# The last output block of a decoder layer: its left half scaled on ScalarE and added in memory to a bias that was stored beforehand

## The chip, the cores and the metric

The kernel runs on one core of one Trainium2 chip. A core has five engines that run their own instruction streams: TensorE (PE in the profile, its weight loads PEld), VectorE (DVE), ScalarE (ACT), GpSimd (POOL) and SyncE (SP, which here only issues transfers). Sixteen DMA engines move data between HBM and the on-chip memory; a transfer is issued from the queue of SP, ACT or POOL. The metric is the device time of one launch in microseconds (us); lower is better. Times of the kernel before: median 613.67 us of three runs (613.48 to 613.99).

## The reference, cut to what matters

One decoder layer with 512 tokens and a model width of 1024: a combined projection, a retention group and a sparse attention group, an output projection with a layer norm, and a gated feed-forward block with a second layer norm. All of it in float32. Only its last lines matter here:

```python
def layer_norm(x, g, b):
    mu = jnp.mean(xf, axis=-1, keepdims=True)
    var = jnp.mean(jnp.square(xf - mu), axis=-1, keepdims=True)
    y = (xf - mu) * lax.rsqrt(var + LN_EPS)
    return (y * g + b)
...
    ffn = (jax.nn.silu(gate) * up) @ w_down
    return layer_norm(DEEPNORM_ALPHA * x + ffn, ln_ffn_gain, ln_ffn_bias)
```

Each output element is `(x - mean) * gain * rstd + bias`, where the mean and `rstd = 1/sqrt(var + eps)` belong to a token (a row), and gain and bias to a column.

## The kernel before

The 512 tokens are four blocks of 128 (`NB = 4`), a token on each of the 128 partitions, and the width of 1024 lies in two halves, `cl` (columns 0 to 511) and `cr` (512 to 1023). A tile `y[b]` of 128x1024 holds the running sum of block `b`; the trace calls it `x`. The tile `gf` (`gbf` in the trace) holds two rows repeated on all partitions: gain in `gf[:, 0]`, bias in `gf[:, 1]`. It is loaded some 40 us before the end. The whole program is scheduled by hand: each engine does its instructions in the order in which the code writes them, and semaphores between engines are set by the framework.

The down projection is accumulated in PSUM. Every product of float32 values is done as three matmuls (`mm3`, lines 94 to 96) from split high and low parts. The left halves of all blocks are finished early. At the end the right halves follow, block after block: for block `b` the products with the last four chunks of weights (`last4`, 24 matmuls) are added into `right[b]` (`dr` in the trace). Then VectorE adds the sum to `y` (`add_to`, line 1377), takes statistics of the right half (`stat`, line 1380), combines them (`moments`, line 1387), and normalizes.

For the blocks 0, 1 and 2, `rstd_of` adds eps on VectorE (line 471) and has GpSimd raise the result to the power -0.5 (line 472). Meanwhile VectorE does `shift_gain` over the 1024 columns (line 1396: subtract the mean, multiply by the gain). Then come two VectorE instructions of 512 columns that multiply by `rstd` and add the bias (line 1578), each followed by its store, issued from SP.

Block 3, the last, has its right half cut into two quarters of 256 columns, so that the first quarter's sum and statistics are done while the matmuls of the second quarter (`dc` in the trace) run. Its root is taken on ScalarE (`rstd_act`, line 1392) while VectorE does `shift_gain`; then VectorE takes the reciprocal (line 1598) and does the scale and bias in two pieces, 640 columns stored from ACT's queue and 384 columns stored from SP's (lines 1600 and 1601). After its last store SP waits for all transfers one after the other (line 1661), and a barrier of all engines ends the program.

GpSimd also issues transfers that add to their destination (`accum_op=ALU.add`). In this kernel these always add one on-chip tile to another, as in `g_sum2` (line 887).

Of the kernel before, what the change touches and what calls it, by code (L numbers as in the profile page):

```python
# [9 lines left out]
F32 = mybir.dt.float32  # L10
F32R = mybir.dt.float32r
I32 = mybir.dt.int32
AF = mybir.ActivationFunctionType
ALU = mybir.AluOpType

P = 128
S = 512
D = 1024
KT = D // P
NB = S // P  # L20
# [33 lines left out]
def hybrid_layer_kernel(ctx: ExitStack, tc: tile.TileContext, xT, x, pos, w0, wf, wt, wo,  # L54
                        wgu, wd, gng, lmg, lmb, lfg, lfb, ident_d, cols_d, masks_d, decay_d, out):
    nc = tc.nc
    V, A, G, T = nc.vector, nc.scalar, nc.gpsimd, nc.tensor
# [5 lines left out]
    sp = ctx.enter_context(tc.tile_pool(name="sp", bufs=6))  # L63
# [15 lines left out]
    def dma(dst, src):  # L79
        nc.sync.dma_start(dst, src)  # L80
# [387 lines left out]
    def rstd_of(var, n):  # L468
        e = sp.tile([P, 4], F32, tag="ve", name="ve")
        r = sp.tile([P, 4], F32, tag="rs", name="rs")  # L470
        V.tensor_scalar(e[:, :n], var, EPS, None, op0=ALU.add)  # L471
        G.tensor_tensor(r[:, :n], e[:, :n], half[:, :n], op=ALU.pow)  # L472
        return r
# [365 lines left out]
    Q = 2 * P  # L839
# [407 lines left out]
    def conv_w(c, k):  # L1247
        if k == 10 and c == 0:
            wprep((c, k), d10)
        else:  # L1250
            t, i = (r5b, 2) if k == 10 else (draw[c, k // 2], 2 * (k % 2))
            wprep((c, k), [t[:, i:i + 2].rearrange("p k c -> p (k c)")])
# [17 lines left out]
    def d_mm(acc, c, m, b, first, last, cs=slice(0, S)):  # L1270
        wh, wl = dw[c, m]
        for k in range(2):
            h, l = dh[m, k]
            bs = slice(b * P, b * P + P)
            ws = slice(k * S + cs.start, k * S + cs.stop)
            mm3(acc, h[:, bs], l[:, bs], wh[:, ws], wl[:, ws], first and k == 0, last and k == 1, skip_group_check=True)
# [92 lines left out]
    y = x1  # L1369
    cl, cr = slice(0, S), slice(S, D)  # L1370
# [5 lines left out]
    def add_to(b, cs, acc):  # L1376
        V.tensor_tensor(y[b][:, cs], y[b][:, cs], acc, op=ALU.add)

    def stat(b, i, cs):
        V.bn_stats(stats[b][:, i], y[b][:, cs])  # L1380
# [4 lines left out]
    def moments(b, n=2):  # L1385
        mv = sp.tile([P, 2], F32, tag="lmv", name="fmv")
        V.bn_aggr(mv, stats[b][:, :n])
        return mv

    def rstd_act(var):  # L1390
        e = sp.tile([P, 4], F32, tag="ve", name="ve")
        A.activation(e[:, :1], var, AF.Sqrt, bias=eps)
        return e

    def shift_gain(b, mv):
        V.scalar_tensor_tensor(y[b], in0=y[b], scalar=mv[:, 0:1], in1=gf[:, 0], op0=ALU.subtract, op1=ALU.mult)

    def prepare_down():
        conv_w(0, 0)
# [82 lines left out]
    gf = None  # L1482
    for i in range(18):
# [26 lines left out]
        elif i == 10:  # L1510
# [3 lines left out]
            gf = big.tile([P, 2, D], F32, tag="s8", name="gbf")  # L1514
# [51 lines left out]
        d_mm(right[b], 1, 10, b, b >= 2, True)  # L1566
    conv_w(1, last4[3])

    for b in range(NB - 1):
        for i in last4:  # L1570
            d_mm(right[b], 1, i, b, False, i == last4[-1])
        add_to(b, cr, right[b])
        stat(b, 1, cr)
        mv = moments(b)
        r = rstd_of(mv[:, 1:2], 1)
        shift_gain(b, mv)
        for cs in (cl, cr):
            V.scalar_tensor_tensor(y[b][:, cs], in0=y[b][:, cs], scalar=r[:, 0:1], in1=gf[:, 1, cs],
                                   op0=ALU.mult, op1=ALU.add)
            dma(out[b * P:(b + 1) * P, cs], y[b][:, cs])  # L1580

    b = NB - 1
    Q2 = slice(Q, S)
# [9 lines left out]
    stat(b, 2, c2)  # L1593
    mv = moments(b, 3)
    e = rstd_act(mv[:, 1:2])
    shift_gain(b, mv)
    r = sp.tile([P, 4], F32, tag="rs", name="rs")
    V.reciprocal(r[:, :1], e[:, :1])
    for cs, queue in ((slice(0, 640), nc.scalar), (slice(640, D), nc.sync)):
        V.scalar_tensor_tensor(y[b][:, cs], in0=y[b][:, cs], scalar=r[:, 0:1], in1=gf[:, 1, cs], op0=ALU.mult, op1=ALU.add)  # L1600
        queue.dma_start(out[b * P:b * P + P, cs], y[b][:, cs])


# [61 lines left out]
```

## Time and profile before

| what | value |
|---|---|
| median of the runs | 613.67 us (613.48 to 613.99) |
| the profiled execution | 613.35 us |
| its span, first to last instruction | 611.6 us |
| outside the span | 1.75 us |
| PE busy | 601.7 us, 98% of the span |
| DVE, ACT, POOL busy | 518.7, 350.6, 182.5 us |
| last matmul starts | 603.90 us |
| last VectorE instruction | 607.70 us |
| last store issued (SP) | 608.34 us, 192 KB, 2.3 us to landing |

Times in rows are counted from the span's start. PE is busy nearly everywhere, so for the most part a stage is worth what it does to PE. The last 7.4 us, after the end of the last matmul, are an exception: there PE has nothing left to do, and VectorE and the stores set the end. In a timeline row stand start, length, engine, line, operation, the output and its inputs, and the shapes; a bracket says how long the engine had been idle and who released it. "SPq", "ACTq" and "POOLq" are the engines' queues, where transfers are issued and waits happen. A transfer's time to landing counts from its issue.

### The profile page before, as it was taken

The page shows a single profiled execution, that of the slowest core. Times are in us where ns is not written, and L with a number is a line of the kernel's source. Part 1 is how long each engine was busy: PE and PEld are TensorE (multiplying, and loading weights), DVE is VectorE, ACT ScalarE, POOL GpSimd, SP SyncE. Part 2 cuts the span into 40 slices and gives each one's busy share as a digit, 9 for nine tenths or more (in the row PEclk, how much of TensorE's full clock was granted, in tenths as well). Part 3 has the DMA queues.
Part 4 walks back from the last instruction along what each step waited for, and adds up shares of the span by engine and source line. Part 5 has one row for each costly group of instructions (what it writes and reads, how often), then busy time and mean ns, then how long its engine had stood idle before and what let it go on. Part 6 is the DMA issues. An engine that isn't in the chain of part 4 may idle for free.

```text
span 611.6 us, 9201 instructions
## 1 busy us (share of the span) xinstructions
PE 601.7 (98%) x3256; PEld 519.1 (85%) x3256; DVE 518.7 (85%) x943; ACT 350.6 (57%) x619; POOL 182.5 (30%) x197
## 2 busy tenths in 40 slices
PE   9999999999999999999999999999999999999995
PEld 7987888888888878889998888888888988888884
DVE  6788976898987887989999989889898878977856
ACT  5454444433352755877757776767777685648300
POOL 0136732331363000342013444435353421214011
PEclk9999999999999999999999999999999999999999
DMA  8875774689553873497248888888878879689602
GB/s 295 239 235 148 156 182 124 151 206 224 135 127 104 295 254 129 113 245 144 87 147 206 179 194 200 176 208 165 208 150 198 178 226 205 155 228 295 201 34 103
DMA packets 48014, 110.77 MB, mean 181 GB/s; under 512 B 8880, under 2 KB 23280, under 8 KB 42464
## 3 DMA queue, kind: packets, MB, share of 16 engines
q1 hardware_dynamic: 25232, 77.02, 38.2%
q0 software_dynamic: 22432, 32.71, 32.0%
q8 instruction: 25, 0.41, 0.3%
q10 hardware_dynamic: 304, 0.46, 0.3%
q14 instruction: 21, 0.17, 0.1%
HBM read 74.52 MB, written 2.10 MB: 125 GB/s over the span
## 4 chain that ended last, share of the span: by engine, by line
PE 86%; DVE 5%; POOL 2%; DMA 2%; issue 2%; ACT 1%; SPq 1%; POOLq 0%; DVEq 0%; ACTq 0%
PE ga L921 10%; PE ga L923 5%; PE gc L921 5%; PE ga L929 5%; PE pt L95 4%; PE pt L94 4%; PE pt L96 3%; PE pf L96 3%; PE pf L94 3%; PE pf L95 3%; PE gc L923 3%; PE gb L921 3%; PE dl L94 2%; PE dl L96 2%; PE dl L95 2%; PE gc L929 2%
## 5 line engine op out<-in xcount | busy, mean ns | idle before, releaser
L86 ACT CAST wh<-raw 128x1024 fp32r<-128x1024 f32 x44 | 46.0, 1048 | 40.6 <-PE pt L96 16.2
L872 POOL DMA_DIRECT2D t<-t x34 | 29.1, 857 | 85.7 <-DVE t L1005 57.3
L94 PE MATMUL pf<-xh,wh 128*128 128x512 f32 x128 | 50.1, 392 | 0.3 <-DVE rt L235 0.3
L96 PE MATMUL pf<-xh,wl 128*128 128x512 f32 x128 | 50.0, 390 | 0.2 <-DMA wl<-raw 0.2
L95 PE MATMUL pf<-xl,wh 128*128 128x512 f32 x128 | 49.9, 390 | 0.0
L872 POOL DMA_DIRECT2D w<-w x34 | 39.0, 1184 | 32.5 <-DVE w L955 23.9
L472 POOL TENSOR_TENSOR rs<-ve,half 128x1 f32<-128x1 f32 (+1 forms) x11 | 11.9, 1083 | 109.4 <-DVE ve L471 109.2
L91 DVE TENSOR_TENSOR wl<-raw,wh 128x1024 fp32r<-128x1024 f32 x26 | 31.6, 1222 | 12.1 <-ACT wh L86 12.0
L94 PE MATMUL pt<-wh,xh 128*128 128x512 f32 (+1 forms) x96 | 38.5, 401 | 0.0
L95 PE MATMUL pt<-wl,xh 128*128 128x512 f32 (+1 forms) x96 | 37.0, 386 | 0.0
L96 PE MATMUL pt<-wh,xl 128*128 128x512 f32 (+1 forms) x96 | 36.7, 382 | 0.0
L89 POOL DMA_DIRECT2D wl<-raw x18 | 15.8, 876 | 49.9 <-ACT wl L88 39.6
L96 PEld LDWEIGHTS pf<-xh,wl 128*128 128x128 f32 x128 | 24.0, 188 | 5.7 <-DMA wl<-raw 0.6
L94 PEld LDWEIGHTS pf<-xh,wh 128*128 128x128 f32 x128 | 24.0, 188 | 5.2 <-issue 0.7
L95 PEld LDWEIGHTS pf<-xl,wh 128*128 128x128 f32 x128 | 24.1, 188 | 4.5
L434 DVE MAX8 m<-score 128x8 f32<-128x256 f32 (+2 forms) x48 | 26.8, 558 | 1.0
L435 DVE MATCH_REPLACE8 score<-m,score 128x256 f32<-128x256 f32 (+2 forms) x48 | 26.0, 542 | 0.0
L417 ACT ACTIVATE lg<-lg 128x256 f32<-128x256 f32 (+2 forms) x24 | 10.9, 474 | 23.1 <-PE lg L416 21.2
L89 POOL DMA_DIRECT2D slot<-hu x9 | 10.9, 1336 | 37.9 <-ACT slot L88 37.2
L96 PEld LDWEIGHTS pt<-wh,xl 128*128 128x128 f32 x96 | 18.0, 188 | 3.3
L423 DVE SCALAR_TENSOR_TENSOR score<-lg,iw,score 128x256 f32<-128x256 f32 (+2 forms) x21 | 13.0, 618 | 9.2 <-ACT lg L417 8.2
L94 PEld LDWEIGHTS pt<-wh,xh 128*128 128x128 f32 x96 | 18.1, 188 | 2.8
(1184 smaller groups left out, 1984.1 us busy)
## 6 DMA issues: line engine op xcount, KB each, us to landing
graw<-in_wgu_dram SPq DMA_DIRECT2D x22, 1024.0 KB, 5.4
wl<-raw POOLq DMA_DIRECT2D x18, 512.0 KB, 5.2
raw<-in_wo_dram SPq DMA_DIRECT2D x8, 1024.0 KB, 4.9
raw<-in_wf_dram SPq DMA_DIRECT2D x7, 1024.0 KB, 6.5
raw<-in_wt_dram SPq DMA_DIRECT2D x6, 1024.0 KB, 5.1
r<-in_wd_dram SPq DMA_DIRECT2D x12, 512.0 KB, 5.8
w<-w POOLq DMA_DIRECT2D x34, 128.0 KB, 4.0
graw<-graw POOLq DMA_DIRECT2D x17, 256.0 KB, 3.7
```

The costliest lines, as they stand in the source:

```text
L86: A.copy(hi, src)
L89: nc.gpsimd.dma_start(lo.bitcast(F32), src, accum_op=ALU.add)
L91: eng_lo.tensor_tensor(lo, src, hi.bitcast(F32), op=ALU.subtract)
L94: T.matmul(acc, lhsT=lh, rhs=rh, start=first, stop=False, **kw)
L95: T.matmul(acc, lhsT=lh, rhs=rl, start=False, stop=False, **kw)
L96: T.matmul(acc, lhsT=ll, rhs=rh, start=False, stop=last, **kw)
L434: V.max(m8, a)
L435: V.match_replace(out=a, in_to_replace=m8, in_values=a, imm_value=TAKEN)
L872: nc.gpsimd.dma_start(t[:, :Q], t[:, Q:], accum_op=ALU.add)
L921: T.matmul(pair, lhsT=h[:, ws[k]], rhs=parts[q][:, :, k], start=first and k == 0, stop=False, skip_group_check=True)
L923: T.matmul(full[:, :Q], lhsT=l[:, ws[k]], rhs=parts[q][:, 0, k], start=False, stop=k == 3, skip_group_check=True)
L929: T.matmul(gp[n][acc], lhsT=a[:, i * S + k * P:i * S + k * P + P], rhs=parts[q][:, b, k], start=first and j == 0, stop=j == 11, skip_group ...
```

## The change

The left half of the last block no longer gets its bias on VectorE:

- Once `gf` is there, before the last blocks, SP stores the bias rows of the left half straight into the last block's left half of the output.
- Block 3's `shift_gain` is cut into halves. After the left half comes the reciprocal; then ScalarE multiplies the left half by `rstd` (a `Copy` with a scale per partition), and GpSimd issues a transfer that adds it to the stored bias, in HBM.
- Meanwhile VectorE does `shift_gain` on the right half, and scale and bias in two quarters of 256 columns, stored from ACT's queue and from SP's.
- Block 2 takes its root on ScalarE and the reciprocal on VectorE as block 3 does, not on GpSimd.

```diff
-    def shift_gain(b, mv):
-        V.scalar_tensor_tensor(y[b], in0=y[b], scalar=mv[:, 0:1], in1=gf[:, 0], op0=ALU.subtract, op1=ALU.mult)
+    def shift_gain(b, mv, cs=slice(0, D)):
+        V.scalar_tensor_tensor(y[b][:, cs], in0=y[b][:, cs], scalar=mv[:, 0:1], in1=gf[:, 0, cs], op0=ALU.subtract, op1=ALU.mult)
+
+    def inverse(e):
+        r = sp.tile([P, 4], F32, tag="rs", name="rs")
+        V.reciprocal(r[:, :1], e[:, :1])
+        return r
+
+    def scale_bias(b, r, cs, queue):
+        V.scalar_tensor_tensor(y[b][:, cs], in0=y[b][:, cs], scalar=r[:, 0:1], in1=gf[:, 1, cs], op0=ALU.mult, op1=ALU.add)
+        queue.dma_start(out[b * P:(b + 1) * P, cs], y[b][:, cs])
...
+    last = out[(NB - 1) * P:NB * P, cl]
+    dma(last, gf[:, 1, cl])
     for b in range(NB - 1):
...
-        r = rstd_of(mv[:, 1:2], 1)
-        shift_gain(b, mv)
+        if b == NB - 2:
+            e = rstd_act(mv[:, 1:2])
+            shift_gain(b, mv)
+            r = inverse(e)
+        else:
+            r = rstd_of(mv[:, 1:2], 1)
+            shift_gain(b, mv)
...
-    shift_gain(b, mv)
-    r = sp.tile([P, 4], F32, tag="rs", name="rs")
-    V.reciprocal(r[:, :1], e[:, :1])
-    for cs, queue in ((slice(0, 640), nc.scalar), (slice(640, D), nc.sync)):
-        V.scalar_tensor_tensor(y[b][:, cs], in0=y[b][:, cs], scalar=r[:, 0:1], in1=gf[:, 1, cs], op0=ALU.mult, op1=ALU.add)
-        queue.dma_start(out[b * P:b * P + P, cs], y[b][:, cs])
+    shift_gain(b, mv, cl)
+    r = inverse(e)
+    A.activation(y[b][:, cl], y[b][:, cl], AF.Copy, scale=r[:, 0:1])
+    nc.gpsimd.dma_start(last, y[b][:, cl], accum_op=ALU.add)
+    shift_gain(b, mv, cr)
+    for cs, queue in ((slice(S, S + Q), nc.scalar), (slice(S + Q, D), nc.sync)):
+        scale_bias(b, r, cs, queue)
```

How the instructions move on VectorE, after the last statistics of block 3 (`x_1_1956` is the tile of the last two blocks, `ve` the root, `rs` its reciprocal):

```order
 L1387 BN_AGGR fmv<-fst_2775 128x2
-L1396 SCALAR_TENSOR_TENSOR x_1_1956<-x_1_1956,fmv,gbf 128x1024
-L1598 RECIPROCAL rs<-ve 128x1
-L1600 SCALAR_TENSOR_TENSOR x_1_1956<-x_1_1956,rs,gbf 128x640
-L1600 SCALAR_TENSOR_TENSOR x_1_1956<-x_1_1956,rs,gbf 128x384
-L1661 UNCONDITIONAL_BRANCH
+L1396 SCALAR_TENSOR_TENSOR x_1_1956<-x_1_1956,fmv,gbf 128x512
+L1400 RECIPROCAL rs<-ve 128x1
+L1396 SCALAR_TENSOR_TENSOR x_1_1956<-x_1_1956,fmv,gbf 128x512
+L1404 SCALAR_TENSOR_TENSOR x_1_1956<-x_1_1956,rs,gbf 128x256 x2
```

The reciprocal now comes after 512 columns and not after 1024, and 512 columns of scale and bias remain on VectorE where there were 1024.

On GpSimd's queue, after the last transfers of the down projection (`slot`):

```order
 L89 DMA slot_5741<-ts_5236 128x512
-L472 TENSOR_TENSOR rs<-ve,half 128x1 x3
-L1661 UNCONDITIONAL_BRANCH
-L1661 ISA
+L472 TENSOR_TENSOR rs<-ve,half 128x1 x2
+L1613 DMA out_dram<-x_1_1956 128x512
+L1676 UNCONDITIONAL_BRANCH
+L1676 ISA
```

One of GpSimd's three powers is gone, and a transfer is its last work before the end of the program.

On SP's queue, from the last loads of weights (`draw`) on:

```order
 L80 DMA draw_1_5769<-in_wd_dram 128x2x512 x2
-L80 DMA out_dram<-x_0_1955 128x512 x4
-L80 DMA out_dram<-x_1_1956 128x512 x2
-L1601 DMA out_dram<-x_1_1956 128x384
-L1661 UNCONDITIONAL_BRANCH
+L80 DMA out_dram<-gbf 128x512
+L1405 DMA out_dram<-x_0_1955 128x512 x4
+L1405 DMA out_dram<-x_1_1956 128x512 x2
+L1405 DMA out_dram<-x_1_1956 128x256
```

The store of the bias stands behind the last loads and ahead of all other stores.

More of the change, by code (lines that the diff above doesn't have):

```diff
@@ L1574, in hybrid_layer_kernel @@
         mv = moments(b)
-        r = rstd_of(mv[:, 1:2], 1)
-        shift_gain(b, mv)
+        if b == NB - 2:
[5 more added lines that the diff above has]
+            shift_gain(b, mv)
         for cs in (cl, cr):
-            V.scalar_tensor_tensor(y[b][:, cs], in0=y[b][:, cs], scalar=r[:, 0:1], in1=gf[:, 1, cs],
-                                   op0=ALU.mult, op1=ALU.add)
-            dma(out[b * P:(b + 1) * P, cs], y[b][:, cs])
+            scale_bias(b, r, cs, nc.sync)
     b = NB - 1
```

## The prediction

> **What bounds the kernel now.** I looked at the core's span and clock first, then at the timeline after the last matmul, since only that part of the program is rewritten.
>
> ```profile
> core 0: 611.6 us, clock 0.998
> ```
>
> The clock is full, so no row below is stretched by the throttle. The timeline of the end (start, length, engine, line):
>
> ```profile
> 603.90 0.28 PE L96 MATMUL dc<-dh(1, 3)_5888,h 128*128 128x256 f32 x1
> 603.99 0.43 DVE L1380 BATCH_NORM_STATS2 fst<-x 128x6 f32<-128x256 f32 x1
> 604.33 0.41 DVE L1377 TENSOR_TENSOR x<-x,dc 128x256 f32<-128x256 f32 x1
> 604.77 0.43 DVE L1380 BATCH_NORM_STATS2 fst<-x 128x6 f32<-128x256 f32 x1
> 605.23 0.24 DVE L1387 BATCH_NORM_AGGREGATE fmv<-fst 128x2 f32<-128x18 f32 x1
> 605.50 1.28 DVE L1396 SCALAR_TENSOR_TENSOR x<-x,fmv,gbf 128x1024 f32<-128x1024 f32 x1
> 605.56 0.30 ACT L1392 ACTIVATE ve<-fmv,eps 128x1 f32<-128x1 f32 x1 [22.37 <-DVE fmv L1387]
> 606.71 0.16 DVE L1598 RECIPROCAL rs<-ve 128x1 f32<-128x1 f32 x1
> 606.90 1.42 DVE L1600 SCALAR_TENSOR_TENSOR x<-x,rs,gbf 128x640 f32<-128x640 f32 x2
> 607.82 0.38 ACTq L1601 DMA_DIRECT2D out_dram<-x  x1
> 608.34 0.33 SPq L1601 DMA_DIRECT2D out_dram<-x  x1
> ```
>
> VectorE is busy without a gap from 603.99 to 608.32, and the last store leaves 0.02 us after it. The transfers of that stretch and who waits for them:
>
> ```profile
> out_dram<-x SPq DMA_DIRECT2D x6, 256.0 KB, 2.0
> out_dram<-x ACTq DMA_DIRECT2D x1, 320.0 KB, 2.2
> out_dram<-x SPq DMA_DIRECT2D x1, 192.0 KB, 2.3
> ...
> SPq L1661 <- DMA out_dram<-x: 1.4, 2, 0.9
> ```
>
> The last store lands at 608.34 + 2.3 = 610.64, and SP has waited for it; the 0.96 us from there to 611.6 are the closing barrier. So the end is "last transfer landed + 0.96", and a term below counts only if it moves that landing.
>
> **The change part by part.**
>
> *The store of the bias.* 256 KB from SP, behind the last loads.
>
> ```profile
> 561.87 7.62 SPq L80 DMA_DIRECT2D draw<-in_wd_dram  x4
> 591.86 0.35 SPq L80 DMA_DIRECT2D out_dram<-x  x1
> ...
> 576.70 1.06 ACT L86 CAST dh(1, 2)_5860<-draw 128x1024 fp32r<-128x1024 f32 x1 [1.66 <-PE dr L96]
> ```
>
> SP's queue has over 20 us free between the last load and the first store, and ScalarE's conversions of these loads wait for PE's buffers, not for the loads. At 2.0 us a store is in HBM well before 591. Cost 0; without that cover it would be at most its 2.0 us.
>
> *Block 2's root on ScalarE.* The rows of block 2:
>
> ```profile
> 598.04 0.39 PE L96 MATMUL dr<-dh(1, 3)_5888,h 128*128 128x512 f32 x1
> 598.47 0.69 DVE L1377 TENSOR_TENSOR x<-x,dr 128x512 f32<-128x512 f32 x1 [0.55 <-PE dr L96]
> ...
> 600.16 0.15 DVE L471 TENSOR_SCALAR ve<-fmv 128x1 f32<-128x1 f32 x1
> 600.23 1.28 DVE L1396 SCALAR_TENSOR_TENSOR x<-x,fmv,gbf 128x1024 f32<-128x1024 f32 x1
> 600.46 1.45 POOL L472 TENSOR_TENSOR rs<-ve,half 128x1 f32<-128x1 f32 x1 [3.99 <-DVE ve L471]
> 601.94 1.41 DVE L1578 SCALAR_TENSOR_TENSOR x<-x,rs,gbf 128x512 f32<-128x512 f32 x2 [0.44 <-POOL rs L472]
> ```
>
> Without line 471, `shift_gain` starts at 600.16 and ends at 601.44; ScalarE's root (0.30 us after a 0.1 us handover) is hidden under it; the reciprocal takes 0.16 us, overlapping as at 606.71. Scale and bias then start near 601.56, 0.38 us earlier. Of that only a part arrives: the addition of `dc` waits for the matmul that ends at 603.90 + 0.28 = 604.18. With the handover of 0.04 us from PE (598.43 to 598.47) it starts at 604.22 and not at 604.33. **Gain 0.11 us.** The rest becomes a wait for PE.
>
> *Block 3 on VectorE.* The shapes of these instructions, grouped:
>
> ```profile
> L1578 DVE SCALAR_TENSOR_TENSOR x<-x,rs,gbf 128x512 f32<-128x512 f32 x6 | 4.2, 749 | 1.3 <-POOL rs L472 1.3
> L1600 DVE SCALAR_TENSOR_TENSOR x<-x,rs,gbf 128x640 f32<-128x640 f32 x1 | 0.9, 886 | 0.0
> L1600 DVE SCALAR_TENSOR_TENSOR x<-x,rs,gbf 128x384 f32<-128x384 f32 x1 | 0.6, 614 | 0.0
> ```
>
> 256 columns more cost 272 ns, so 512 columns take 0.75 us and 256 columns 0.48 us; independent neighbours overlap by 0.07 us. With 0.11 off every start, `shift_gain` of the left half runs 605.39 to 606.14, the reciprocal ends at 606.23, `shift_gain` of the right half ends at about 606.95, and the quarters end at 607.46 and 607.87. SP's last store therefore leaves at 607.89, 0.45 us earlier than 608.34, and would land at 610.2.
>
> *ScalarE's scaling.* No row shows a 512-column copy with a scale per partition. The nearest:
>
> ```profile
> L886 ACT ACTIVATE graw<-graw 128x512 f32<-128x512 f32 x17 | 10.8, 634 | 2.8 <-DVE gs L880 2.8
> L593 ACT ACTIVATE ast<-ast,mx 128x512 f32<-128x512 f32 x4 | 2.8, 723 | 0.0
> ```
>
> The first has a constant scale, the second an operand per partition: 0.63 to 0.72. I take 0.71. From the reciprocal 606.23 plus the 0.09 us that line 1392 needed after VectorE, it runs 606.32 to 607.03. VectorE to GpSimd took 0.15 us (600.31 to 600.46); the same here puts GpSimd's transfer at **607.18**. Behind it on GpSimd is only the end of the program.
>
> *The accumulating store.* All transfers of this kind in the trace add tile to tile on the chip. The one with the least beside it is that of line 887, issued at 319.87; its window 318:324 shows the rate in slices of 0.15 us and the time to landing:
>
> ```profile
> GB/s 55 0 0 109 0 0 0 0 0 0 0 0 0 68 184 184 143 198 96 0 0 27 191 205 205 191 191 205 191 218 123 0 0 0 437 0 109 218 109 0
> ...
> graw<-graw POOLq DMA_DIRECT2D x1, 256.0 KB, 3.3
> ```
>
> 1.3 us until bytes move, 1.4 us at some 200 GB/s, 0.5 us until it counts as landed: 3.3 us for 256 KB, against 2.0 for the plain store. Two things are added here. First, company: two plain stores of 128 KB at the rate of the present stores in the window 606:611,
>
> ```profile
> GB/s 0 0 0 0 0 0 0 0 0 0 0 0 0 0 0 0 0 0 0 0 0 164 369 369 410 430 369 410 324 369 369 381 222 12 0 0 0 0 0 0
> ```
>
> some 370 GB/s, so 0.7 us of all DMA engines; bytes move from 608.5 to 610.0 for the accumulating store, about 608.6 to 609.9 for these, so nearly all may fall on it. 0 to 0.7; I take 0.5. Second, the destination is read from HBM. The nearest row is a load of the same size:
>
> ```profile
> r2a<-in_wd_dram SPq DMA_DIRECT2D x1, 256.0 KB, 2.8
> ```
>
> If reading only lengthens the pipe, it costs what that load takes over a store, 2.8 - 2.0 = 0.8 at most, and perhaps nothing; if all of it came ahead of the addition, 2.8. I take 0.4, near the pipelined end, since the on-chip addition shows its two inputs streamed at a steady rate. Sum: 3.3 + 0.5 + 0.4 = **4.2 us**, bounds 3.3 and 6.8.
>
> So the accumulating store lands at 607.18 + 4.2 = 611.4, after SP's (610.2) and 0.75 us after what is last today. The half on ScalarE is ready 1.16 us before today's last issue, and the slower road gives back 1.9. **Sum: +0.75 us.** The profiled execution would take 613.35 + 0.75 = 614.1; the median of the runs lies 0.32 above that execution, hence 614.4.
>
> The Trainium skill ("DMA: Bandwidth & Descriptors", "Anatomy of one DMA — SWDGE (gpsimd) path") gives a transfer issued from GpSimd about 2.0 us plus its bytes at 436 GB/s. That would be 2.6 us here; line 887 took 3.3, and its steady 200 GB/s is the difference, so the trace disagrees for accumulating transfers. By the page the store lands at 609.8, SP's store is last, and the time is 613.2. The same page ("Issuing engines are not separate DMA queues") says that transfers from all queues share the same 16 DMA engines and interleave, which speaks against a third queue at the very end. The present two stores, from ACT and SP, agree: together they keep the 370 GB/s of one. By that rule the company term is the full 0.7, the landing 611.6, and the time 614.6.
>
> **Rivals.**
>
> *Hidden (0.15).* The accumulating store costs 3.3 or a little less and lands at 610.5 or before; SP's store, 610.2, or both set the end: -0.15 to -0.45 us, 613.2 to 613.5. For it: the rate of line 887 is steady. Against it: HBM must be read, and two stores lie beside it.
>
> *Serial reading from HBM (0.20), the slower side.* If the addition waits for its data from HBM, packet by packet, the store takes 3.3 + 2.8 = 6.1 us and lands at 613.3: +2.6, so 616.3. It decides from an issue-to-landing time of 4.7 on (608.34 + 2.3 + 1.23 - 607.18), where the loss passes 0.2%. For it: no transfer of this kind to HBM is in the trace. Against it: the pipelining above.
>
> *GpSimd's own closing takes over (0.20).* The rows of the end of the program have this one:
>
> ```profile
> L1661 POOLq EVENT_SEMAPHORE  x4: 17/17/17, 610.8 to 611.4; - x4
> L1661 POOLq DRAIN  x3: 46/98/4955, 600.4 to 611.3; - x3
> ```
>
> The first drain starts at 600.4 together with the last power, and lasts 4.96 us, 3.5 beyond the power's end at 601.91. Now it is hidden: it ends at 605.4, and GpSimd's first step of the barrier is at 610.8. Issuing a transfer keeps GpSimd busy for 0.86 us,
>
> ```profile
> 319.87 0.86 POOL L887 DMA_DIRECT2D graw<-graw  x1 [0.41 <-ACT graw L886]
> ```
>
> so with one as last work at 607.18 the drain ends at 611.5 (608.04 + 3.5) to 612.1 (607.18 + 4.96), and the barrier is held 0.7 to 1.3 us: 614.4 to 615.0. This would hold whatever the store takes. Against it: two later drains of GpSimd last 0.05 and 0.1 us, so the length of the first may belong to the power ahead of it.
>
> **How the numbers follow.** Forecast 0.45, hidden 0.15, serial 0.20, closing 0.20. The measurement cannot tell less than about 0.2% (1.23 us) from no change, 612.44 to 614.90. Faster by more than that needs more than the whole 0.45 of VectorE and the most favourable transfer: 0.04 of the hidden case. Within: the forecast but for 0.03, the rest of the hidden case, half of the closing case: 0.42 + 0.11 + 0.10 = 0.63. Slower: 0.03 + 0.20 + 0.10 = 0.33. The range leaves out the extreme of the serial case and half of the unlikely gain: 613.1 to 616.0; the forecast's own is 613.6 to 615.0.
>
> **What would show it.** ScalarE's 512-column row at about 0.71 us and GpSimd's transfer issued at about 607.2; VectorE's last instruction ending near 607.9; the accumulating store's time to landing (4.2; below 3.5 it is the hidden case, above 4.7 the serial one); SP's last wait for it and not for the plain stores; GpSimd's drain ending before or after that landing. Block 2's scale should start near 601.6, and the addition of `dc` at 604.2, released by PE. The forecast is wrong if the store to HBM is as quick as a plain one, or if the drain, or anything ahead of 603.9, moves the end.

## The result

The changed kernel is slower: a median of 616.56 us against 613.58 us of the kernel before in the same comparison, a ratio of 1.0051 with a 95% interval of 1.0041 to 1.0061. That is 3.0 us, outside the predicted range of 613.1 to 616.0 and on its upper side. The profiled execution took 615.75 us, with this span:

```profile
core 0: 614.0 us, clock 0.995
```

The mean clock is a little lower than the 0.998 before, but not where PE works: up to 604 us the granted clock is 1.00 in both profiles, and only in the idle end it is 0.71 here and 0.83 before.

The end of the changed kernel in the timeline, from the last matmul on:

```profile
603.86 0.28 PE L96 MATMUL dc<-dh(1, 3)_5888,h 128*128 128x256 f32 x1
604.17 0.42 DVE L1377 TENSOR_TENSOR x<-x,dc 128x256 f32<-128x256 f32 x1 [0.19 <-PE dc L96]
...
605.37 0.75 DVE L1396 SCALAR_TENSOR_TENSOR x<-x,fmv,gbf 128x512 f32<-128x512 f32 x1
606.03 0.16 DVE L1400 RECIPROCAL rs<-ve 128x1 f32<-128x1 f32 x1
606.11 0.73 DVE L1396 SCALAR_TENSOR_TENSOR x<-x,fmv,gbf 128x512 f32<-128x512 f32 x1
606.23 0.72 ACT L1612 ACTIVATE x<-x,rs 128x512 f32<-128x512 f32 x1 [0.56 <-DVE rs L1400]
606.87 0.88 DVE L1404 SCALAR_TENSOR_TENSOR x<-x,rs,gbf 128x256 f32<-128x256 f32 x2
607.24 0.90 POOL L1613 DMA_DIRECT2D out_dram<-x  x1 [10.81 <-ACT x L1612]
607.39 0.38 ACTq L1405 DMA_DIRECT2D out_dram<-x  x1
607.78 0.33 SPq L1405 DMA_DIRECT2D out_dram<-x  x1
```

The last matmul starts at 603.86, where it started at 603.90 before, so everything ahead of the end took the same time in these two profiles, and the whole 2.4 us of the spans' difference lies behind it. VectorE's last instruction ends at 607.75, 0.57 us earlier than before; SP's last store leaves 0.56 us earlier. Yet the end is later. The transfers of this end, from issue to landing:

```profile
out_dram<-x POOLq DMA_DIRECT2D x1, 256.0 KB, 4.2
out_dram<-x ACTq DMA_DIRECT2D x1, 128.0 KB, 1.9
out_dram<-x SPq DMA_DIRECT2D x1, 128.0 KB, 2.0
```

The plain stores have landed by 609.8; the accumulating one lands at 607.24 + 4.2 = 611.4. But the barrier does not follow it by 0.2 us, as it followed the last landing before (610.64, then GpSimd's first step at 610.8). The rows of the program's closing line, and last the row of SP's drain in the kernel before:

```profile
L1676 POOLq EVENT_SEMAPHORE  x4: 17/17/17, 613.3 to 613.9; - x4
L1676 SPq DRAIN  x3: 7/7/7, 611.8 to 613.5; - x3
L1676 POOLq DRAIN  x3: 46/98/5993, 607.2 to 613.7; - x3
...
L1661 SPq DRAIN  x3: 7/7/7, 610.7 to 611.0; - x3
```

(name and count, then shortest/median/longest length in ns, then the first and the last start.) GpSimd's first drain, which stands right behind its transfer, starts at 607.2 and lasts 5.99 us, to 613.2. SP has seen all landings and reaches its own drain at 611.8; GpSimd takes its first step of the barrier at 613.3, where it was at 610.8 before. This is 2.5 us, the whole difference. Not all of it is the drain. SP's own drain came 0.1 us after the last landing before and comes 0.4 us after it here (the reason is shown with the version in three pieces). So the later landing makes 0.8 us of the difference, SP's longer waits 0.3, and GpSimd's drain, for which the barrier stands from 611.8 on, 1.3. The list of who waited for whom on SP's queue has it as two rows:

```profile
SPq L1676 <- DMA out_dram<-x: 3.1, 2, 1.6
SPq L1676 <- PEq L1676: 2.0, 2, 1.5
```

The first is the wait for landings, the longest 1.6 us. The second is the barrier: SP stands in it for 1.5 us although no engine has work left. It is put down to PE, which is only the last name in the barrier; the row of GpSimd's drain shows who was late.

### The profile page after: what moved, and what is told of

Its sections match the earlier page's. It is cut to its first block, busy times and chain, and to the rows that moved or that the text cites. A ratio compares the mean times of both kernels' runs of the same rounds, so it can differ in the third digit from the quotient of the medians.

```text
span 614.0 us, 9204 instructions
## 1 busy us (share of the span) xinstructions
PE 601.4 (98%) x3256; PEld 519.1 (85%) x3256; DVE 518.8 (85%) x944; ACT 352.0 (57%) x621; POOL 182.0 (30%) x197
## 4 chain that ended last, share of the span: by engine, by line
PE 85%; DVE 6%; issue 3%; DMA 2%; ACT 1%; SPq 1%; POOL 0%; POOLq 0%; ACTq 0%; DVEq 0%
PE ga L921 10%; PE ga L923 5%; PE gc L921 5%; PE ga L929 5%; PE pt L95 4%; PE pt L94 3%; PE pt L96 3%; PE pf L94 3%; PE pf L96 3%; PE pf L95 3%; PE gc L923 3%; PE gb L921 3%; PE dl L96 2%; PE dl L94 2%; PE dl L95 2%
## 5 line engine op out<-in xcount | busy, mean ns | idle before, releaser
L472 POOL TENSOR_TENSOR rs<-ve,half 128x1 f32<-128x1 f32 (+1 forms) x10 | 10.5, 1054 | 105.8 <-DVE ve L471 105.7
```

## The experiments

A measure first. What lies before the last matmul does not take the same time in every execution (the last matmul of the profiles below starts anywhere from 603.2 to 605.7, in the two profiles of the change at 603.86 and 605.73), so spans of two profiles cannot be compared to some tenths. What was edited lies behind the last matmul, and I compare the **tail**: the span's end minus the start of the last matmul. The kernel before has 611.55 - 603.90 = 7.65 us, the change 613.99 - 603.86 = 10.13. Each tail is that of one profile; the two of the change differ by 0.07 us, so a difference of 0.1 us is not to be relied on.

| kernel | tail, us | drain ends after GpSimd's last work, us | after its transfer's landing, us | ratio to before (95%) |
|---|---|---|---|---|
| before | 7.65 | 3.5 (a power) | - | |
| the change | 10.13 | 5.1 | 1.8 | 1.0051 (1.0041 to 1.0061) |
| the change again | 10.20 | 5.1 | 1.8 | 1.0049 (1.0035 to 1.0062) |
| block 2's root alone | 7.56 | over early | - | 1.0008 (0.9999 to 1.0017) |
| plain store from SP | 7.31 | over early | - | 1.0004 (0.9994 to 1.0014) |
| before + late power | 7.85 | 3.5 | - | 1.0009 (0.9999 to 1.0018) |
| before + late small transfer | 8.20 | 3.5 | 2.5 | 1.0003 (0.9993 to 1.0013) |
| plain store from GpSimd | 8.94 | 4.1 | 1.8 | 1.0019 (1.0008 to 1.0029) |
| 64 KB added in HBM | 8.95 | 3.9 | 1.8 | 1.0027 (1.0017 to 1.0038) |
| added on the chip | 9.90 | 4.8 | 1.8 | 1.0038 (1.0023 to 1.0053) |
| one block earlier | 7.55 | over early | 1.8 | 1.0005 (0.9995 to 1.0015) |
| three pieces | 7.92 | over early | - | 1.0008 (0.9999 to 1.0017) |

**Block 2's root alone.** Added to the kernel before:

```diff
-        r = rstd_of(mv[:, 1:2], 1)
-        shift_gain(b, mv)
+        if b == NB - 2:
+            e = rstd_act(mv[:, 1:2])
+            shift_gain(b, mv)
+            r = sp.tile([P, 4], F32, tag="rs", name="rs")
+            V.reciprocal(r[:, :1], e[:, :1])
+        else:
+            r = rstd_of(mv[:, 1:2], 1)
+            shift_gain(b, mv)
```

> The kernel before with one part of the change alone: block 2 takes its root on ScalarE and its reciprocal on VectorE, not on GpSimd. Theory (GpSimd's closing drain after its late transfer costs the time): this part is innocent; block 2's scale starts near 601.5, the addition of dc near 604.2, the last store 0.1 us earlier, so 0.1 us less than before, which is not to be told from no change. Rival (moving the root disturbs something ahead of the end): up to 3 us more than before.

Measured: a tail of 7.56 us, 0.09 less than before, hardly more than two profiles of one kernel differ by; in the runs no difference that can be told. This part of the change does not cost the 2.5 us.

**The change with a plain store from SP.** It leaves the bias of that half out of the output.

```diff
-    nc.gpsimd.dma_start(last, y[b][:, cl], accum_op=ALU.add)
+    dma(last, y[b][:, cl])
```

> The change with its accumulating store replaced by a plain store from SP of the half that ScalarE scaled, so the bias of the left half of the last block is left out. Theory: GpSimd has no work after block 1, its drain is over long before the end, SP's last store leaves near 607.8 and lands near 610.0; 0.5 to 0.7 us less than before (about 613.0), some 3.5 us less than the change. Rival 1 (three stores at the end hinder each other): the last lands later than 610.6, no less than before. Rival 2 (the 3 us come from ScalarE's part, the split or the early bias store): near 616, as the change.

Measured: a tail of 7.31 us, 0.34 less than before and 2.8 less than the change. The split of VectorE's work, ScalarE's scaling, the early store of the bias and three stores at the end are all still in it, so the loss hangs on the one transfer from GpSimd. Its last work is the power of block 1, in the profile's rows for GpSimd and for the closing line:

```profile
594.92 1.46 POOL L472 TENSOR_TENSOR rs<-ve,half 128x1 f32<-128x1 f32 x1 [3.97 <-DVE ve L471]
...
L1676 POOLq EVENT_SEMAPHORE  x4: 17/17/17, 610.4 to 611.0; - x4
L1676 POOLq DRAIN  x3: 46/98/4955, 594.9 to 610.8; - x3
```

The same drain of 4.96 us ends at 599.9 here, and the barrier starts at 610.4. In the runs the 0.34 us are not to be told from no change.

**The kernel before with a late power on GpSimd, and with a late small transfer.** Each adds two lines behind the last reciprocal:

```diff
+    spare = sp.tile([P, 4], F32, tag="spare", bufs=1, name="spare")
+    G.tensor_tensor(spare[:, :1], r[:, :1], half[:, :1], op=ALU.pow)
```

> The kernel before with one more power of one column on GpSimd, of the last block's reciprocal, written to a spare tile; no transfer is added. It starts near 607.0 and ends near 608.5. Theory A (the drain is long after whatever GpSimd did last, 3.5 us beyond a power as in the kernel before): the drain ends near 612.0 and the barrier starts 1.1 us later, 1.1 to 1.2 us more than before. Theory B (only a transfer from GpSimd makes the drain at the end matter, and the 5 us before had another cause): no change.

```diff
+    spare = sp.tile([P, 4], F32, tag="spare", bufs=1, name="spare")
+    nc.gpsimd.dma_start(spare[:, :1], r[:, :1])
```

> The kernel before with one small plain transfer from GpSimd (one column, 128 words, on the chip, to a spare tile) that waits for the last block's reciprocal, so it is issued near 607.0. It lands within some 2 us, near 609. Theory A1 (the drain takes a fixed 5 us from the end of GpSimd's work of issuing): the drain ends near 613.0, 2.2 us more than before, though the transfer is small and neither goes to HBM nor adds. Theory A2 (the drain waits for the transfer to land and then 1.8 us, as in the change: 613.2 after a landing at 611.4): it ends near 610.8, no change. Rival (only accumulation to HBM costs): no change.

The late power's rows (GpSimd's timeline, then the closing line):

```profile
607.75 0.54 POOL L1600 TENSOR_TENSOR spare<-rs,half 128x1 f32<-128x1 f32 x1 [5.03 <-DVE rs L1598]
...
L1663 POOLq EVENT_SEMAPHORE  x4: 17/17/17, 611.8 to 612.5; - x4
L1663 POOLq DRAIN  x3: 46/97/4058, 607.7 to 612.3; - x3
```

The drain ends at 607.72 + 4.06 = 611.8, that is 3.5 us after the power's end at 608.3, exactly as far as in the kernel before (601.91 to 605.39). GpSimd enters the barrier as soon as it is over. So theory A holds in its mechanism: 3.5 us after GpSimd's last work, whatever it was. Its price was put too high, since the power took 0.54 us and not 1.45 (why it is shorter here was not tried): the drain ended only just after the last landing, and the tail grew by 0.20 us, not by 1.1.

The late small transfer's rows (timeline, the transfer's landing, closing line):

```profile
606.46 0.61 POOL L1600 DMA_DIRECT2D spare<-rs  x1 [5.26 <-DVE rs L1598]
...
spare<-rs POOLq DMA_DIRECT2D x1, 0.5 KB, 1.7
...
L1663 POOLq EVENT_SEMAPHORE  x4: 17/17/17, 610.7 to 611.3; - x4
L1663 POOLq DRAIN  x3: 46/98/4178, 606.4 to 611.1; - x3
```

The drain ends at 610.6. A fixed 5 us from the end of the issuing (607.07) would have given 612.1, a landing at 608.2 plus 1.8 would have given 610.0; it is 3.5 us after the issuing again. SP was at its own drain at 610.0, so the barrier waited for GpSimd, and the tail grew by 0.55 us; the runs (1.0003) do not tell that from nothing. Neither A1 nor A2 was right by itself. What fits all drains so far is the later of two times: 3.5 us after GpSimd's last work, and, in the change, 1.8 us after its transfer has landed. Three kernels were then made to tell that from its rivals.

**Which property of the transfer counts.** Each replaces the accumulating store of the change: by a plain one of the same size, by one of a quarter of the columns, and by one that adds on the chip. Each leaves the bias out of all or part of that half of the output.

```diff
-    nc.gpsimd.dma_start(last, y[b][:, cl], accum_op=ALU.add)
+    nc.gpsimd.dma_start(last, y[b][:, cl])
```

> The change with its accumulating store replaced by a plain store of the same 256 KB from GpSimd, so the bias of the left half of the last block is left out. So far GpSimd's drain ended 3.5 us after its last work in three kernels (two powers, one small transfer), but 5.1 us after it in the change. Theory L (the drain also waits for the transfer to land, and ends 1.8 us after that, as in the change: 611.4 to 613.2): landing near 610.4, drain to 612.2, span near 613.0. Theory A (adding costs the extra 1.5 us): drain to 611.6, span near 612.4. Theory S (256 KB of transfer cost it, whatever they do): drain to 613.2, span 614.0.

```diff
-    nc.gpsimd.dma_start(last, y[b][:, cl], accum_op=ALU.add)
+    nc.gpsimd.dma_start(last[:, :P], y[b][:, :P], accum_op=ALU.add)
+    dma(last[:, P:], y[b][:, P:S])
```

> The change with only 128 of the 512 columns added in HBM by GpSimd (64 KB); the other 384 are stored plainly from SP without their bias, so that part of the output lacks it. Theory L (drain ends 1.8 us after the landing, or 3.5 us after GpSimd's last work, whichever is later): landing near 610.0, drain to 611.6 to 611.8, span near 612.5. Theory A (any adding transfer costs 1.5 us more): drain to 613.2, span 614.0. Theory S (the amount): drain to 611.6.

```diff
-    nc.gpsimd.dma_start(last, y[b][:, cl], accum_op=ALU.add)
+    nc.gpsimd.dma_start(gf[:, 1, cl], y[b][:, cl], accum_op=ALU.add)
+    dma(last, y[b][:, cl])
```

> The change with GpSimd's transfer adding the scaled half to the bias tile on the chip and not to the output in HBM; SP stores the scaled half plainly, so the bias of the left half of the last block is left out of the output. Theory L: landing 3.3 to 4.0 us after 607.2, near 611.0, drain to 612.8, span near 613.6. Theory A or S: drain to 613.2, span 614.0. Theory H (only HBM as destination matters): drain to 611.6, span 612.4.

The rows of the three (GpSimd's timeline, landing, drain), first the plain store:

```profile
607.46 0.63 POOL L1613 DMA_DIRECT2D out_dram<-x  x1 [10.81 <-ACT x L1612]
...
out_dram<-x POOLq DMA_DIRECT2D x1, 256.0 KB, 3.0
...
L1676 POOLq DRAIN  x3: 46/98/4789, 607.4 to 612.7; - x3
```

Then the addition of 64 KB in HBM:

```profile
608.46 0.90 POOL L1613 DMA_DIRECT2D out_dram<-x  x1 [10.81 <-ACT x L1612]
...
out_dram<-x POOLq DMA_DIRECT2D x1, 64.0 KB, 3.0
...
L1677 POOLq DRAIN  x3: 46/98/4805, 608.4 to 613.8; - x3
```

And the addition on the chip:

```profile
608.51 0.89 POOL L1613 DMA_DIRECT2D gbf<-x  x1 [10.81 <-ACT x L1612]
...
gbf<-x POOLq DMA_DIRECT2D x1, 256.0 KB, 3.9
...
L1677 POOLq DRAIN  x3: 46/98/5761, 608.5 to 614.8; - x3
```

Landings at 610.4, 611.4 and 612.4; ends of the first drain (its start plus its longest length) at 612.2, 613.2 and 614.3. By the trace's unrounded times the drain ends 1.81 us after the landing each time, and so it does in the two profiles of the change. Plain or adding, 64 or 256 KB, HBM or on the chip make no difference beyond the landing itself. (The last matmul was later than the change's 603.86: 604.07 with the plain store, 605.08 and 605.13 with the other two, so the expected times are to be read 0.2 and 1.2 later.) That is theory L. A and S fall with the plain store: its issuing ended at 608.09, from which the 3.5 us of A give 611.6 and the 5.1 us of S 613.2, and it was 612.2; H falls with the addition on the chip, whose drain ended 4.8 us after the issuing and not 3.5.

**The same device one block earlier.** The edit of the changed kernel, cut to its core (block 3 is as in the kernel before):

```diff
-    last = out[(NB - 1) * P:NB * P, cl]
+    last = out[(NB - 2) * P:(NB - 1) * P, cl]
...
-        for cs in (cl, cr):
-            scale_bias(b, r, cs, nc.sync)
+        if b == NB - 2:
+            A.activation(y[b][:, cl], y[b][:, cl], AF.Copy, scale=r[:, 0:1])
+            nc.gpsimd.dma_start(last, y[b][:, cl], accum_op=ALU.add)
+        else:
+            scale_bias(b, r, cl, nc.sync)
+        scale_bias(b, r, cr, nc.sync)
```

> The same device one block earlier: the bias of block 2's left half is stored beforehand, that half is scaled on ScalarE and added in HBM by GpSimd; block 3 is done as in the kernel before. Theory (the loss of the change is GpSimd's closing drain after a late transfer and nothing else): the transfer leaves near 602.4, lands near 606.6, the drain ends near 608.4 and is hidden; the end is that of the kernel with block 2's root alone moved, barrier near 610.7, 0.1 us less than before: no change to be told. Rival (an accumulating store to HBM disturbs the rest, or the early bias store does): 2 us or more above before.

```profile
603.78 0.90 POOL L1595 DMA_DIRECT2D out_dram<-x  x1 [6.10 <-ACT x L1594]
...
out_dram<-x POOLq DMA_DIRECT2D x1, 256.0 KB, 3.6
...
L1677 POOLq EVENT_SEMAPHORE  x4: 17/17/17, 611.9 to 612.6; - x4
L1677 POOLq DRAIN  x3: 46/98/5477, 603.8 to 612.4; - x3
```

The transfer and its drain are as long as ever, but the drain is over at 609.2, again 1.81 us after its own transfer's landing and long before the last plain store has landed (611.8), so it is GpSimd's own transfer that counts. The tail is 7.55 us, that of the root alone. Issued nearly 5 us earlier against the last matmul, the same accumulating store costs nothing that can be measured. (The absolute times are 1.2 us later than expected because the last matmul of this execution started at 605.11.)

**The change again, and a version in three pieces.** The first has no edit. The second is the kernel with the root alone moved and this:

```diff
-    for cs, queue in ((slice(0, 640), nc.scalar), (slice(640, D), nc.sync)):
+    for cs, queue in ((slice(0, 384), nc.scalar), (slice(384, 768), nc.sync), (slice(768, D), nc.scalar)):
```

> The change itself once more, unaltered. From the last matmul's start to the end of the span the kernel before takes 7.65 us and the change 10.13. Theory L (GpSimd's drain ends 1.8 us after its transfer has landed): again about 10.1, with the drain's end 1.8 us after the landing, whatever the stage before the last matmul does; 2.4 to 3.0 us above before in the runs. Rival (the drain of the first profile was an accident of that execution): a tail between 8 and 9 us, and the loss of the runs is to be looked for elsewhere.

> A version without GpSimd at the end: the kernel with block 2's root moved to ScalarE, and the last block's scale and bias in three pieces of 384, 384 and 256 columns, stored from ACT, SP and ACT. VectorE ends 0.14 us later for the extra piece, but the first store leaves 0.27 us earlier and the last has 128 KB and not 192. Theory (the landing of the last store and then the barrier set the end): a tail of 7.3 to 7.5 us against 7.56 of the kernel with the root alone moved; in the runs no change to be told from before. Rival (the 16 DMA engines are what is full at the end, 512 KB in 1.4 us): 7.56 or a little more.

The change repeats itself: a tail of 10.20, with the drain from 609.1 for 6.05 us, though its last matmul started 1.9 us later than in the first profile.

```profile
L1676 POOLq DRAIN  x3: 46/98/6052, 609.1 to 615.7; - x3
```

The three pieces were a miss: 7.92, which is 0.36 more than two pieces with the root alone moved. The last store of the three, in the timeline, the transfers and the closing line:

```profile
608.11 0.34 ACTq L1607 DMA_DIRECT2D out_dram<-x  x1
...
out_dram<-x ACTq DMA_DIRECT2D x1, 128.0 KB, 2.1
...
L1667 SPq DRAIN  x3: 7/7/7, 610.7 to 611.0; - x3
```

And that of the two pieces:

```profile
608.19 0.33 SPq L1607 DMA_DIRECT2D out_dram<-x  x1
...
out_dram<-x SPq DMA_DIRECT2D x1, 192.0 KB, 2.3
...
L1667 SPq DRAIN  x3: 7/7/13, 610.6 to 610.9; - x3
```

With three pieces the last landing is at 608.11 + 2.1 = 610.2, with two at 608.19 + 2.3 = 610.5. Counted from the last matmul (603.63 and 603.85) both are 6.6 us: the smaller last piece left 0.14 us later and took 0.2 us less, so it landed hardly sooner. Whether full DMA engines have a part in that, as the rival had it, the runs do not show. The loss lies behind the landing: SP reaches its own drain 0.1 us after it with two pieces and 0.5 us after it with three. SP checks the transfers' semaphores in ten waits, one after the other, a step about each 0.06 us, and the trace's records of these waits show where the time goes. With three pieces the wait for the store that lands last is the third of the ten and ends at 610.27, with seven more to follow; with two pieces it is the tenth. In the change the wait for GpSimd's transfer is the fourth. In every kernel here with three or more final stores SP's drain comes 0.4 to 0.5 us after the last landing, in every one with two 0.1. A list in another order was not tried. No version tried beats the kernel before by more than can be measured.

## Why the prediction was wrong

*Right, step by step.* Block 2's root: scale and bias of block 2 start at 601.51 (forecast 601.56), and the addition of `dc` waits for PE and starts at 604.17. VectorE's pieces: 0.75, 0.73 and 0.48 us, as taken from the slope of two rows. ScalarE's scaling: 0.72 us against 0.71. GpSimd's transfer: issued at 607.24 against 607.18. The early store of the bias, issued at 570.26, costs nothing, as the plain store from SP and the early block show (its row is loaded at 560.97, some 50 us before the end and not 40). And the sum for the accumulating store, the most uncertain term, came out at 4.2 us and a landing of 611.4, both as forecast. Its parts are less sure than the sum. On the chip the transfer took 3.3 us alone (line 887) and 3.9 beside three plain stores of 512 KB in all; to HBM it took 3.6 with one plain store of 256 KB just ahead of it (one block earlier) and 4.2 beside the change's two, also 256 KB. So HBM costs about 0.3 in both comparisons (taken as 0.4) and company about 0.6 (taken as 0.5), but no two of these had the same company, and that the sum agrees to 0.1 us is in part luck. The serial rival is excluded: the HBM addition is 0.3 us longer, not 2.8. So is the hidden case. The estimate of 2.6 us from the formula in the Trainium skill ("DMA: Bandwidth & Descriptors", "Anatomy of one DMA — SWDGE (gpsimd) path") was exceeded by every transfer of this size from GpSimd named here: 3.0 for the plain store beside two others, 3.3 to 4.2 for the adding ones.

*Wrong: the step that the end is "last transfer landed + 0.96".* It was read from an end with two stores, from ACT and SP, and holds there; in the change the end came 2.6 us after the landing (611.4 to 614.0). For a transfer from GpSimd there is a second way to the barrier, GpSimd's own drain, and it ends 1.8 us after the landing, where SP's way took 0.1 us before and takes 0.4 here. That is the rival "GpSimd's own closing takes over", to which 0.20 was given. It was the right mechanism with too small a price: it was sized on the two readings that one row allowed, 3.5 us after the last work or 4.96 us from its start, with the sum 614.4 to 615.0, and it was said to hold whatever the store takes. Both readings belong to a GpSimd whose last work is a computation. The measured price is the third, the landing plus 1.8: 613.2 and not 611.5 to 612.1. So what the store takes counts after all.

*The account of the profile.* The landing is 0.8 us later than before (611.4 against 610.6), as forecast. Before, GpSimd's first step of the barrier came 0.2 us after the landing, here 1.9. Of these further 1.7 us, 0.3 belong to SP's waits, whose order the prediction did not look at: without GpSimd's drain the barrier would still have stood until 611.8. The drain holds it for 1.3 more. Together that is 2.4 of the 2.5 us by which the tails differ.

*What stays open.* In the runs the loss is 3.0 us both times, and the tails explain 2.5. These 2.5 us lie at the lower edge of the first interval (1.0041) and inside the second (1.0035). The profiled execution of the change was the fastest of its six, 0.8 us below their median, where that of the kernel before lies 0.2 below. Several variants whose tails are shorter than that of the kernel before also measured up to 0.08% above it; whether an edit at the end changes the time ahead of the last matmul, or chance does, was not settled.

The chances were 0.33 for slower by more than 0.2%, and half of the closing case was counted as no change. Had the price of the drain been bounded from above by "landing plus something", as the unknown wait deserved, the case would have stood wholly on the slower side.

## What to carry to other kernels

At the end of a program the store that lands last is not the whole story: each engine must also be done, and in this kernel GpSimd is done late, 3.5 us after its last work and 1.8 us after its last transfer has landed. So give the last 6 us before the end (here 4.2 us to the landing and 1.8 more) to the queues of SP and ACT, and let GpSimd's last transfer go one stage earlier, where the same device cost nothing that could be measured. Count the final stores too: here a third one put 0.3 to 0.4 us between the last landing and the barrier. When a row of the profile shows a long wait that is hidden only because nobody needs that engine, price it from the event that a new last instruction would bring, not from its length today.

## What the runs showed of the hardware that was not expected

- GpSimd's drain behind its last instruction ended 3.5 us after a power (five kernels) or after the issuing of a small transfer (one), and 1.81 us after the landing of a longer transfer (the same to 0.01 us in six executions), whichever was later.
- Adding into HBM instead of into on-chip memory made a 256 KB transfer only about 0.3 us longer (3.3 to 3.6, and 3.9 to 4.2 beside other stores, with company that was not quite the same). In the change's end (606 to 612 us in 40 slices) the bytes of the plain stores move first, at about 300 GB/s, then those of the addition at about 200, the rate of the on-chip one:

```profile
GB/s 0 0 0 0 0 0 0 0 0 0 0 0 0 0 0 232 355 294 294 362 314 116 177 164 205 205 218 191 164 150 28 14 14 0 0 0 0 0 0 0
```

- SP's closing waits cost about 0.06 us each. With three or more final stores 0.4 to 0.5 us passed between the last landing and SP's drain, with two 0.1, because the wait for the last landing then stood third or fourth of ten and not last.
